# Griffin trunk layer on one core: three tiles for the gate chain, earlier steps for h, and m5 ahead of m4 in the last stage

## The chip, the cores and the metric

The kernel runs on one core of one Trainium2 chip. The metric is device time in microseconds (us), the median of several executions. The page of the profile is of one execution.

## The reference

DEPTH is 1, so only the first kind of layer runs, a Griffin recurrent block, on 1024 tokens of width 2048. Cut to what is computed:

```python
u = rmsnorm(x, norm_pre)
proj = u @ w_in                      # (1024, 2048) @ (2048, 4096)
xb, gate = proj[..., :2048], proj[..., 2048:]
xc = causal_depthwise_conv4(xb) + conv_b
r = sigmoid(blockdiag(xc, w_r) + b_r)   # 8 blocks of 256 x 256
i = sigmoid(blockdiag(xc, w_i) + b_i)
log_a = -8 * r * softplus(-lam);  a = exp(log_a)
b = sqrt(-expm1(2 * log_a)) * (i * xc)
h_t = a_t * h_{t-1} + b_t            # scan over the tokens
y = (h * silu(gate)) @ w_out
h = x + rmsnorm(y, norm_post)
out = h + sigmoid(h @ w_gate) * (p @ w_ple)
```

## The kernel before

All tensors lie with features on partitions and tokens along the row, in two halves of 512 tokens (h = 0 and 1 in the names). Every float32 product is made of three matmuls of 128x512 on split operands (`mm3`, lines 116 to 118: hi x hi, hi x lo, lo x hi). A split is one ScalarE (ACT) copy into `whi` or the hi half of an operand (line 106) and one VectorE (DVE) subtraction into `wlo` or the lo half (line 107).

The three large products (x with `w_in`, y with `w_out`, h with `w_gate`) go by Winograd's form of Strassen's scheme: seven products m1 to m7 for each block p of 128 output rows. One product of one block is a **unit**, 8 x 3 = 24 matmuls on TensorE (PE). `grouped` and `led` write out the order of the units: m1 and m2, then m7, m6, m3 in groups of four, then m4 and m5, where `led(a, b, 2, ...)` gives b a lag of two blocks behind a. In the last stage m4 yields one tile of the output (i = 1, h = 0) and m5 two (h = 1), in `emit_out`. m4 reads the operand t4, m5 reads t1; both are differences of spilled tiles that `h_one` loads, subtracts and splits.

The program is a list of steps. `now[0]` counts units. Each unit has stages that are issued some units ahead: LOAD (7 ahead for m5 and m7, 4 for m1, m2 and m4), ADD (a weight block added onto the loaded one by a DMA on the GpSimd (POOL) queue, 5 ahead) and PART (the split, 3 ahead). `hook` and `spread` put other steps behind a unit of a stage, `do` behind the unit that stands before it. `later(k, f)` and `put(key, d, src, k)` issue a store to DRAM k units later on the POOL queue. SP and POOL run in the order in which this is written; from the y stage's third quarter on ACT and DVE do too (`begin_by_hand`), before that a scheduler sets their order and PE's. Each engine and queue works strictly in its order, so an instruction that waits holds up all behind it.

Tiles come from pools: `pairs` (13 buffers: raw weights, sums, output operands), `vecs` (7 buffers of 128x512: `one`), `acts` (24 split operands), and 8 PSUM banks.

**The chain.** For each of 8 blocks n and each half h, `block_conv` makes xc and its split x2, four banks of `ri` matmuls follow (`mm_ri`, a unit of its own), and `chain` makes r, i, a, b and the scan from them. One tile `rq` of 128x3x1024 holds R, I and Q (Q ends as the scan's states). There is one buffer of it. For h = 0 the states are stored by `put(..., 6)` (names `sp<-rq`), for h = 1 they are multiplied with the gate tile g (line 348).

**From y to h.** After the last y products come eight units `ple` (p with `w_ple`, 24 matmuls each, evacuated by ACT into `vecs` tiles pp, line 722, and stored). `h_first(n)` loads two z tiles and x, its use scales and adds them (`make_h`, lines 654 and 656, tile zr), stores the result and splits it into the operands b11 and b21 (names h_b) one unit later. h's first unit, m1 of block 0, reads all eight. `norm_z(step, 1)` is the second half's norm: its step 2 puts eight small matmuls on PE (`rb_z`).

Of the kernel before, what the change touches and what calls it, by code (L numbers as in the profile page):

```python
# [34 lines left out]
def trunk_kernel(ctx, tc, xT, pT, par, w_in, w_ri, w_out, w_gate, w_ple, out):  # L35
# [160 lines left out]
    def later(k, f):  # L196
        late.setdefault(now[0] + k, []).append(f)
# [115 lines left out]
        chain(h, n, banks)  # L313

    def chain(h, n, banks):
        rq = chain_tile("rq", f"rq{h}_{n}", (P, 3, 2, T))
        R, I, Q = (rq[:, j] for j in range(3))
        A2 = st.pop(("xc", h, n))
        for s in range(2):
            ct = 2 * n + s  # L320
            nc.scalar.activation(R[:, s], banks[0][s], AF.Sigmoid, bias=col(C_BR, ct))  # L321
            nc.scalar.activation(I[:, s], banks[1][s], AF.Sigmoid, bias=col(C_BI, ct))
        nc.vector.tensor_tensor(I, I, A2, ALU.mult)
        for s in range(2):
            nc.scalar.activation(Q[:, s], R[:, s], AF.Tanh, scale=dk[:, 0, 2 * n + s : 2 * n + s + 1])

        for s in range(2):
            ct = 2 * n + s
            nc.scalar.activation(R[:, s], R[:, s], AF.Exp, scale=dk[:, 1, ct : ct + 1])
        nc.scalar.activation(R, R, AF.Square)  # L330
        nc.scalar.activation(R, R, AF.Square)
        nc.scalar.activation(A2, R, AF.Square)
        nc.vector.scalar_tensor_tensor(Q, A2, 1.0, Q, op0=ALU.add, op1=ALU.mult)
        root = nc.scalar.activation(Q, Q, AF.Sqrt)
        if h == 1:
            later(2, lambda: open_gates(root.ins))
        nc.vector.tensor_tensor(I, I, Q, ALU.mult)
        for s in range(2):
            ct = 2 * n + s
            init = 0.0 if h == 0 else hcar[:, ct : ct + 1]  # L340
            nc.vector.tensor_tensor_scan(Q[:, s], R[:, s], I[:, s], init, ALU.mult, ALU.add)
        if h == 0:
            nc.vector.tensor_copy(hcar[:, 2 * n : 2 * n + 2], Q[:, :, T - 1])
            for s in range(2):
                put(2 * n + s, hs, Q[:, s], 6)
        else:
            g = gs.pop(n)
            nc.vector.tensor_tensor(g, Q, g, ALU.mult)
            for s in range(2):
                put((("b12", "b22")[s], n), yd, g[:, s], 5)  # L350

# [138 lines left out]
    def strassen(key, w, orders, emit, hooks, early=None, park=False, inserts=()):  # L492
# [14 lines left out]
        def mm(u, p, name):  # L507
# [7 lines left out]
            if name == "m1":  # L515
                banks[p] = b
                if park:
                    m1 = one(f"m1{key}{p}")
                    nc.scalar.activation(m1, b, AF.Copy)
                    put(p, parked, m1, 2)  # L520
                else:
                    u_tile(p)
                    nc.scalar.activation(us[key, p][:, 0], b, AF.Copy)
# [59 lines left out]
    def x_mm(u, p, name):  # L583
# [23 lines left out]
        elif name == "m4":  # L607
# [3 lines left out]
            def gated():  # L611
                nc.scalar.activation(g, g, AF.Silu)
                nc.vector.tensor_tensor(g, g, h0.pop(p), ALU.mult)  # L613
                put((("b11", "b21")[s], n), yd, g)

            gate(gated, p >= NK - 4)
        elif name == "m5":
# [115 lines left out]
    def emit_out(p, i, h, b, part):  # L733
        dt = 2 * p + i
        o, sg = outs.pop((dt, h)), one(f"sg{dt}_{h}")
        if part is None:
            nc.scalar.activation(sg, b, AF.Sigmoid)
        else:
            nc.vector.tensor_tensor(sg, part, b, ALU.subtract if h == 0 else ALU.add)  # L739

        def rest():
            if part is not None:
                nc.scalar.activation(sg, sg, AF.Sigmoid, scale=-1.0 if (i, h) == (0, 1) else 1.0)
            nc.vector.tensor_tensor(sg, sg, o[:, 0], ALU.mult)
            nc.vector.tensor_tensor(sg, sg, o[:, 1], ALU.add)  # L745
            later(1, lambda: nc.gpsimd.dma_start(out[h, :, dt, :], sg))  # L746

        return rest

# [134 lines left out]
    for i in range(3):  # L884
        hook(i, lambda i=i: norm_z(i, 0))
    spread(1, 2, [lambda n=n: h_first(n) for n in range(3)], 2)
    hook(4, lambda: load_p(0))
    hook(5, lambda: load_p(1))
    strassen("y", w_out, [(p, "m5") for p in range(NB)], emit_z, hooks)
    uses = {}  # L890
    for i in range(KH):
        plain(w_ple[i], f"ple{i}", lambda u, i=i: mm_ple(u, i), 512)
        for f in uses.pop(i, ()):
            do(f)
        if i < 5:
            got = []
            do(lambda got=got, i=i: got.append(h_first(i + 3)))
            uses.setdefault(i + 2, []).append(lambda got=got: got.pop()())
        if i < 3:
            do(lambda i=i: norm_z(i, 1))  # L900


    orders, o2, o3 = grouped(range(NB), range(NB), led("m4", "m5", 2, range(NB)))
    hooks = {}
    spread(0, 1.5, [lambda n=n: h_second(n) for n in range(KH)], 2)
    spread(o2 - 1, 0.75, fetches("h", hold, "t2"), 2)
    spread(o2 + 2, 0.75, [lambda n=n: fetch("h", {("b22", k): hd[1, 2 * k + 1] for k in (n, n + 1)}, "b22", n) for n in range(0, KH, 2)], 2)
    spread(o3 - 8, 0.5, [lambda n=n: h_one("t4", n) for n in range(KH)], 2)
    spread(o3 - 4, 0.5, [lambda n=n: h_one("t1", n) for n in range(KH)], 2)
    strassen("h", w_gate, orders, emit_out, hooks, early_out, True)  # L910


# [97 lines left out]
```

## Time and profile before

| | us |
|---|---|
| median of 3 runs (1418.79 to 1422.9) | 1420.37 |
| the profiled execution, its own time | 1417.82 |
| its span, first to last instruction | 1416.0 |
| PE busy | 1380.6 |
| DVE busy | 947.1 |
| ACT busy | 729.5 |
| POOL busy | 271.8 |

Time is lost where PE, in its order, waits; so the table is read together with the list of PE's waits and the stretches around them. The profiled execution is 2.55 us below the median.

### The profile page before, as it was taken

To read this page: it belongs to the slowest core of one execution; us is meant where nothing else is said; L and a number is where in the kernel's file an instruction comes from. 1 tells how busy PE (TensorE), PEld (TensorE's weight loads), DVE (VectorE), ACT (ScalarE), POOL (GpSimd) and SP (SyncE) were. 2 spreads that over 40 slices of the span, in tenths; PEclk is the share of its full clock that TensorE was granted. 3 is DMA by queue.
4 is the path that set the end of the run, shared out by engine and by line. 5 is a ranking of instruction groups with operands and counts; after the bars stand their busy time and mean duration, and the time that the engine had idled before them with its cause. 6 is when DMAs were issued, how large, how long until landed. Compare 5 with 4: busy or idle time off the path is not lost. (4 is left out here: it accounts for less than half of the span.)

```text
span 1416.0 us, 17194 instructions
## 1 busy us (share of the span) xinstructions
PE 1380.6 (97%) x6025; PEld 1128.1 (80%) x6025; DVE 947.1 (67%) x1255; ACT 729.5 (52%) x960; POOL 271.8 (19%) x422
## 2 busy tenths in 40 slices
PE   9999999999999999999999999999999899999997
PEld 6888778778887878888787788888887788888786
DVE  8588678557575656588789855355676586626867
ACT  8332256666666643789898652224345333423423
POOL 0003331112121111011102331102114233110122
PEclk9999999999999999999999999999999999999999
DMA  9778898768777798468776999757589999986995
GB/s 353 241 241 305 297 308 241 217 157 225 186 173 207 189 327 253 159 189 269 242 249 257 336 311 301 186 150 212 131 298 349 325 356 330 301 225 170 317 351 201
DMA packets 126391, 358.81 MB, mean 253 GB/s; under 512 B 15968, under 2 KB 16352, under 8 KB 126304
## 3 DMA queue, kind: packets, MB, share of 16 engines
q1 hardware_dynamic: 83808, 210.88, 42.1%
q0 software_dynamic: 42496, 146.83, 40.0%
q8 instruction: 47, 0.77, 0.2%
q14 instruction: 40, 0.33, 0.1%
HBM read 277.95 MB, written 79.69 MB: 253 GB/s over the span
## 5 line engine op out<-in xcount | busy, mean ns | idle before, releaser
L436 POOL DMA_DIRECT2D x_m<-in_w_in x64 | 57.8, 964 | 190.5 <-DVE wlo_x10m L107 21.1
L294 DVE SCALAR_TENSOR_TENSOR xc<-xbp,cst,xc 128x512 f32<-128x512 f32 x96 | 66.8, 743 | 1.0 <-ACT xc L291 0.9
L436 POOL DMA_DIRECT2D h_m<-in_w_gate x32 | 28.6, 894 | 139.4 <-DVE h_t L107 22.9
L117 PE MATMUL ri<-x,whi_ri 128*128 128x512 f32 x128 | 51.8, 405 | 1.8 <-DVE x L107 1.6
L116 PE MATMUL ri<-x,whi_ri 128*128 128x512 f32 x128 | 49.7, 408 | 3.7 <-ACT x L106 3.7
L118 PE MATMUL ri<-x,wlo_ri 128*128 128x512 f32 x128 | 51.3, 401 | 0.0
L206 POOL DMA_DIRECT2D sp<-g x32 | 17.9, 574 | 164.4 <-DVE g L613 137.0
L321 ACT ACT_TABLE_LOAD x16 | 20.5, 1283 | 51.2 <-DMA sp<-rq 35.0
L436 POOL DMA_DIRECT2D y_m<-in_w_out x32 | 28.3, 895 | 79.5 <-DVE wlo_y4m L107 16.5
L106 ACT ACTIVATE x<-xc 128x1024 fp32r<-128x1024 f32 x16 | 16.8, 1053 | 32.6 <-DVE xc L294 32.6
L116 PEld LDWEIGHTS ri<-x,whi_ri 128*128 128x128 f32 x128 | 24.5, 194 | 10.7 <-ACT x L106 5.0
L291 ACT ACTIVATE xc<-xbp,cst 128x512 f32<-128x512 f32 x32 | 24.4, 806 | 15.5 <-DMA xbp<-sp 12.0
L117 PEld LDWEIGHTS ri<-x,whi_ri 128*128 128x128 f32 x128 | 24.7, 193 | 9.4 <-DVE x L107 3.5
L746 POOL DMA_DIRECT2D out_t<-sg x32 | 18.0, 562 | 69.2 <-DVE sg L745 68.3
L118 PEld LDWEIGHTS ri<-x,wlo_ri 128*128 128x128 f32 x128 | 24.5, 192 | 5.9
L722 ACT ACTIVATE pp<-pp 128x512 f32<-128x512 f32 x32 | 18.1, 596 | 20.7 <-DMA sp<-pp 13.1
L106 ACT ACTIVATE x_t<-xu 128x512 fp32r<-128x512 f32 x8 | 5.0, 630 | 43.1 <-DVE xu L362 43.1
L206 POOL DMA_DIRECT2D sp<-ux x16 | 9.7, 605 | 89.8 <-DVE ux L605 89.6
L107 DVE TENSOR_TENSOR x_t<-fxt,x_t 128x512 fp32r<-128x512 f32 x24 | 15.9, 687 | 16.3 <-ACT x_t L106 16.3
L106 ACT ACTIVATE x_t<-fxt 128x512 fp32r<-128x512 f32 x24 | 14.2, 622 | 23.2 <-DMA fxt<-sp 23.2
L116 PE MATMUL pp<-p,whi_ple 128*128 128x512 f32 x64 | 25.1, 392 | 0.0
L117 PE MATMUL pp<-p,whi_ple 128*128 128x512 f32 x64 | 24.9, 389 | 0.0
(719 smaller groups left out, 4907.3 us busy)
## 6 DMA issues: line engine op xcount, KB each, us to landing
x_m<-in_w_in SPq DMA_DIRECT2D x72, 512.0 KB, 5.8
x_m<-in_w_in POOLq DMA_DIRECT2D x64, 512.0 KB, 7.6
y_m<-in_w_out SPq DMA_DIRECT2D x40, 512.0 KB, 6.7
h_m<-in_w_gate SPq DMA_DIRECT2D x40, 512.0 KB, 8.3
y_m<-in_w_out POOLq DMA_DIRECT2D x32, 512.0 KB, 8.3
o<-sp SPq DMA_DIRECT2D x64, 256.0 KB, 7.7
h_m<-in_w_gate POOLq DMA_DIRECT2D x32, 512.0 KB, 8.6
raw_ri<-in_w_ri SPq DMA_DIRECT2D x16, 512.0 KB, 6.1
```

The costliest lines, as they stand in the source:

```text
L106: nc.scalar.activation(hi, src, AF.Copy)
L107: nc.vector.tensor_tensor(lo, src, hi.bitcast(F32), ALU.subtract)
L116: nc.tensor.matmul(ps, whi, ahi, start=start, stop=False, skip_group_check=more)
L117: nc.tensor.matmul(ps, whi, alo, start=False, stop=False, skip_group_check=more)
L118: nc.tensor.matmul(ps, wlo, ahi, start=False, stop=stop, skip_group_check=more)
L206: nc.gpsimd.dma_start(t, src)
L291: nc.scalar.activation(xc[:, s], xbp[:, s, 3 : T + 3], AF.Identity, bias=col(C_CB, ct), scale=col(C_CW + 48, ct))
L294: nc.vector.scalar_tensor_tensor(xc[:, s], xbp[:, s, j : j + T], col(C_CW + 16 * j, ct), xc[:, s], op0=ALU.mult, op1=ALU.add)
L321: nc.scalar.activation(R[:, s], banks[0][s], AF.Sigmoid, bias=col(C_BR, ct))
L436: nc.gpsimd.dma_start(u["raw"], w[(p, *ADDED[name])], accum_op=ALU.add)
L722: nc.scalar.activation(t, b, AF.Copy)
L746: later(1, lambda: nc.gpsimd.dma_start(out[h, :, dt, :], sg))
```

## The change

1. `chain` takes three tiles (`rr`, `ri`, `rq`) for R, I and Q in place of one. They have the same total size, one buffer each.
2. Stores move to later units: of g of the chain from 5 to 6 for blocks 0 to 5, of m1 of the y and h stages (`parked`) from 2 to 3, of the gated g of m4 in the x stage from 1 to 3 for p below 12.
3. `h_first` for n = 3 and 4 is issued within the y stage (hooks 6 and 7) and used behind ple units 0 and 1. Each use issues the load of n + 2. So all of n = 3 to 7 stand two units earlier. `norm_z(1, 1)` stays behind ple unit 1, its last step (`rb_z`) moves from behind unit 2 to behind unit 3.
4. In the last stage `led("m5", "m4", ...)`: m5 of block p now leads m4 by two blocks. `h_one("t1")` is spread from o3 - 10, `h_one("t4")` from o3 - 6 (o3 is the number of the stage's first m4 or m5 unit); before, t4 from o3 - 8 and t1 from o3 - 4.
5. The last stores of the output (blocks 6 and 7, of m4 and m5) are issued on SP in place of POOL.

```diff
     def chain(h, n, banks):
-        rq = chain_tile("rq", f"rq{h}_{n}", (P, 3, 2, T))
-        R, I, Q = (rq[:, j] for j in range(3))
+        R, I, Q = (chain_tile(t, f"{t}{h}_{n}") for t in ("rr", "ri", "rq"))
         A2 = st.pop(("xc", h, n))
...
-                put((("b12", "b22")[s], n), yd, g[:, s], 5)
+                put((("b12", "b22")[s], n), yd, g[:, s], 6 if n < NB - 2 else 5)
...
-                    put(p, parked, m1, 2)
+                    put(p, parked, m1, 3)
...
-                put((("b11", "b21")[s], n), yd, g)
+                put((("b11", "b21")[s], n), yd, g, 3 if p < NK - 4 else 1)
...
-            later(1, lambda: nc.gpsimd.dma_start(out[h, :, dt, :], sg))
+            later(1, lambda: (nc.sync if p >= NB - 2 and i + h else nc.gpsimd).dma_start(out[h, :, dt, :], sg))
...
     spread(1, 2, [lambda n=n: h_first(n) for n in range(3)], 2)
+
+    uses, got_h = {}, {}
+    for n in range(3, KH):
+        uses[n - 3] = lambda n=n: (got_h.pop(n)(), got_h.__setitem__(n + 2, h_first(n + 2)) if n + 2 < KH else None)
+    for n in (3, 4):
+        hook(n + 3, lambda n=n: got_h.__setitem__(n, h_first(n)))
     hook(4, lambda: load_p(0))
     hook(5, lambda: load_p(1))
     strassen("y", w_out, [(p, "m5") for p in range(NB)], emit_z, hooks)
-    uses = {}
     for i in range(KH):
         plain(w_ple[i], f"ple{i}", lambda u, i=i: mm_ple(u, i), 512)
-        for f in uses.pop(i, ()):
-            do(f)
-        if i < 5:
-            got = []
-            do(lambda got=got, i=i: got.append(h_first(i + 3)))
-            uses.setdefault(i + 2, []).append(lambda got=got: got.pop()())
-        if i < 3:
-            do(lambda i=i: norm_z(i, 1))
-
-
-    orders, o2, o3 = grouped(range(NB), range(NB), led("m4", "m5", 2, range(NB)))
+        if i in (0, 1, 3):
+            do(lambda i=i: norm_z(min(i, 2), 1))
+        if i in uses:
+            do(uses[i])
+
+
+    orders, o2, o3 = grouped(range(NB), range(NB), led("m5", "m4", 2, range(NB)))
...
-    spread(o3 - 8, 0.5, [lambda n=n: h_one("t4", n) for n in range(KH)], 2)
-    spread(o3 - 4, 0.5, [lambda n=n: h_one("t1", n) for n in range(KH)], 2)
+    spread(o3 - 10, 0.5, [lambda n=n: h_one("t1", n) for n in range(KH)], 2)
+    spread(o3 - 6, 0.5, [lambda n=n: h_one("t4", n) for n in range(KH)], 2)
```

ACT's order at the start of the chain of block 3, second half, before the change; rq holds R, I and Q, ri are the banks, g the gates.

```order
L106 ACTIVATE whi_x11m_5213<-x_m_5020 128x1024
L321 ACT_TABLE_LOAD
L321 ACTIVATE rq_3_5301<-ri_3_00_5273,cst 128x512
L321 ACTIVATE rq_3_5301<-ri_3_01_5274,cst 128x512
L612 ACT_TABLE_LOAD
L612 ACTIVATE g_12_5198<-g_12_5198 128x512
L106 ACTIVATE whi_x14m_5269<-x_m_5208 128x1024
L322 ACT_TABLE_LOAD
L322 ACTIVATE rq_3_5301<-ri_3_10_5275,cst 128x512
L322 ACTIVATE rq_3_5301<-ri_3_11_5276,cst 128x512
L325 ACTIVATE rq_3_5301<-rq_3_5301,dk 128x512 x2
L329 ACT_TABLE_LOAD
```

The same place in the changed kernel, where rr is R, ri_3_5320 is I, ri_3_00 to ri_3_11 are still the banks and rq is Q:

```order
L106 ACTIVATE whi_x11m_5231<-x_m_5036 128x1024
L320 ACT_TABLE_LOAD
L320 ACTIVATE rr_3_5319<-ri_3_00_5291,cst 128x512
L611 ACT_TABLE_LOAD
L611 ACTIVATE g_12_5216<-g_12_5216 128x512
L106 ACTIVATE whi_x14m_5287<-x_m_5226 128x1024
L321 ACT_TABLE_LOAD
L321 ACTIVATE ri_3_5320<-ri_3_10_5293,cst 128x512
L320 ACTIVATE rr_3_5319<-ri_3_01_5292,cst 128x512
L321 ACTIVATE ri_3_5320<-ri_3_11_5294,cst 128x512
L324 ACTIVATE rq_3_5321<-rr_3_5319,dk 128x512 x2
L328 ACT_TABLE_LOAD
```

The work is the same; the first instruction that writes Q's tile now is the tanh, behind all four sigmoids.

DVE's order around the first ple units before the change; zr is the tile of `make_h`, h_b its split operand, n_z the norm's small tiles.

```order
L107 TENSOR_TENSOR h_b_8358<-zr_8210,h_b_8358 128x512
L107 TENSOR_TENSOR h_b_8361<-zr_8210,h_b_8361 128x512
L126 TENSOR_SCALAR n_z_8374<-ss_z_8369 128x4
L107 TENSOR_TENSOR wlo_ple_8431<-raw_ple_8316,whi_ple_8430 128x512
L131 RECIPROCAL n_z_8376<-n_z_8375 128x4
L132 TENSOR_TENSOR n_z_8377<-n_z_8376 128x4
L133 TENSOR_TENSOR n_z_8377<-n_z_8377,n_z_8374 128x4
L134 TENSOR_SCALAR n_z_8377<-n_z_8377 128x4
L135 TENSOR_TENSOR n_z_8376<-n_z_8376,n_z_8377 128x4
L107 TENSOR_TENSOR wlo_ple_8491<-raw_ple_8380,whi_ple_8490 128x512
L654 SCALAR_TENSOR_TENSOR zr_8364<-zr_8364,cst,rstd_z_8062 128x512 x2
L656 TENSOR_TENSOR zr_8364<-zr_8364,xr_3_8365 128x1024
```

The same place in the changed kernel:

```order
L107 TENSOR_TENSOR h_b_8403<-zr_8242,h_b_8403 128x512
L126 TENSOR_SCALAR n_z_8411<-ss_z_8406 128x4
L653 SCALAR_TENSOR_TENSOR zr_8302<-zr_8302,cst,rstd_z_8094 128x512 x2
L655 TENSOR_TENSOR zr_8302<-zr_8302,xr_3_8303 128x1024
L107 TENSOR_TENSOR wlo_ple_8476<-raw_ple_8358,whi_ple_8475 128x512
L107 TENSOR_TENSOR h_b_8479<-zr_8302,h_b_8479 128x512
L107 TENSOR_TENSOR h_b_8482<-zr_8302,h_b_8482 128x512
L131 RECIPROCAL n_z_8413<-n_z_8412 128x4
L132 TENSOR_TENSOR n_z_8414<-n_z_8413 128x4
L133 TENSOR_TENSOR n_z_8414<-n_z_8414,n_z_8411 128x4
L134 TENSOR_SCALAR n_z_8414<-n_z_8414 128x4
L135 TENSOR_TENSOR n_z_8413<-n_z_8413,n_z_8414 128x4
```

Block 3's zr steps and splits moved ahead of the norm's chain from line 131 on; the norm's chain keeps its unit.

ACT's order at the start of the last stage before the change; h_t1k is the split of t1 of block k, whi_h0m5 the weights of m5 of block 0, sg the outputs.

```order
L106 ACTIVATE whi_h0m5_10563<-h0_m5_10331 128x1024
L743 ACTIVATE sg1_0_10561<-sg1_0_10561 128x512
L106 ACTIVATE h_t12_10570<-ht1_2_10420 128x512
L106 ACTIVATE h_t13_10573<-ht1_3_10423 128x512
L106 ACTIVATE whi_h3m4_10609<-h3_m4_10531 128x1024
L743 ACTIVATE sg3_0_10607<-sg3_0_10607 128x512
L106 ACTIVATE h_t14_10616<-ht1_4_10472 128x512
L106 ACTIVATE h_t15_10619<-ht1_5_10475 128x512
L106 ACTIVATE whi_h1m5_10663<-h1_m5_10431 128x1024
L743 ACTIVATE sg5_0_10661<-sg5_0_10661 128x512
L106 ACTIVATE h_t16_10670<-ht1_6_10519 128x512
L106 ACTIVATE h_t17_10673<-ht1_7_10522 128x512
```

The splits of t1 in the changed kernel:

```order
L106 ACTIVATE h_t12_10334<-ht1_2_10204 128x512
L106 ACTIVATE h_t13_10337<-ht1_3_10207 128x512
L106 ACTIVATE whi_h6m3_10378<-h6_m7_9908 128x1024
L106 ACTIVATE h_t14_10382<-ht1_4_10245 128x512
L106 ACTIVATE h_t15_10385<-ht1_5_10248 128x512
L106 ACTIVATE whi_h7m3_10423<-h7_m7_9942 128x1024
L106 ACTIVATE h_t16_10427<-ht1_6_10294 128x512
L106 ACTIVATE h_t17_10430<-ht1_7_10297 128x512
L106 ACTIVATE whi_h0m5_10476<-h0_m5_10252 128x1024
```

All of t1 now stands ahead of the split of m5's first weights; before, six of its eight splits stood behind it.

## Rows read from the trace of the kernel before

**Rows 1.** The page, part 1: busy us, share of the span, instructions.
```profile
PE 1380.6 (97%) x6025; PEld 1128.1 (80%) x6025; DVE 947.1 (67%) x1255; ACT 729.5 (52%) x960; POOL 271.8 (19%) x422
```

**Rows 2.** Waits of PE: who waited for whom, us in total, times, longest.
```profile
PE ri L116 <- ACT x L106: 3.7, 3, 2.9
PE hm L116 <- ACT h_b L106: 3.2, 1, 3.2
...
PE rb_z L141 <- ACT pp L722: 2.2, 1, 2.2
...
PE ri L117 <- DVE x L107: 1.6, 2, 1.2
PE hm L117 <- DVE h_t L107: 1.4, 1, 1.4
...
PE hm L117 <- DVE h_b L107: 0.8, 1, 0.8
...
PE hm L116 <- ACT h_t L106: 0.5, 1, 0.5
```

**Rows 3.** Windows: PE, PEld, DVE, ACT, POOL busy (count), PEclk, DMA share, GB/s.
```profile
686.30:692.10 5.80, 5.80 (x14) 4.54 (x15) 5.80 (x7) 2.86 (x4) 0.00 (x0) 0.50 0.45 95
1102.70:1108.90 6.20, 6.20 (x15) 4.85 (x16) 1.74 (x2) 1.54 (x2) 0.90 (x2) 0.51 0.95 328
1110.00:1116.20 6.20, 6.20 (x29) 5.15 (x28) 1.23 (x1) 1.55 (x2) 0.54 (x1) 1.00 0.93 282
```

**Rows 4.** Groups of ACT: busy, mean ns, idle before, what ended it.
```profile
L321 ACT ACTIVATE rq<-ri,cst 128x512 f32<-128x512 f32 x32 | 20.9, 686 | 0.2
L321 ACT ACT_TABLE_LOAD x16 | 20.5, 1283 | 51.2 <-DMA sp<-rq 35.0 <-DVE g L348 16.2
```

**Rows 5.** Timeline of PE, first half's chains: start us, duration [idle before, releaser].
```profile
270.50 0.50 PE L118 MATMUL xm<-x_t,wlo_x4m 128*128 128x512 f32 x1 [2.25 <-DVE wlo_x4m L107]
293.54 0.50 PE L118 MATMUL xm<-x_t,wlo_x7m 128*128 128x512 f32 x1 [0.52 <-DVE wlo_x7m L107]
312.71 0.50 PE L118 MATMUL xm<-x_t,wlo_x6m 128*128 128x512 f32 x1 [1.63 <-DVE wlo_x6m L107]
450.87 0.50 PE L118 MATMUL xm<-x_t,wlo_x15m 128*128 128x512 f32 x1 [1.14 <-DVE wlo_x15m L107]
```

**Rows 6.** Timeline of DVE and ACT, second half, start of block 3's chain.
```profile
655.09 2.46 DVE L341 TENSOR_TENSOR_SCAN rq<-rq,hcar 128x512 f32<-128x512 f32 x2
658.04 1.22 DVE L348 TENSOR_TENSOR g<-rq,g 128x1024 f32<-128x1024 f32 x1
659.36 1.28 ACT L321 ACT_TABLE_LOAD   x1 [1.43 <-DVE g L348]
```

**Rows 7.** Timeline of DVE, PE and ACT around the ple units.
```profile
1064.68 0.16 DVE L135 TENSOR_TENSOR n_z<-n_z,n_z 128x4 f32<-128x4 f32 x1
1064.99 1.13 PE L141 MATMUL rb_z<-ident,n_z 128*128 128x128 f32 x8 [2.23 <-ACT pp L722]
1098.18 1.23 DVE L656 TENSOR_TENSOR zr<-zr,xr 128x1024 f32<-128x1024 f32 x1
1100.63 1.16 ACT L106 ACTIVATE h_b<-zr 128x512 fp32r<-128x512 f32 x2
```

**Rows 8.** Timeline of ACT, last stage.
```profile
1331.42 1.06 ACT L106 ACTIVATE whi_h3m<-h_m 128x1024 fp32r<-128x1024 f32 x1 [5.07 <-DMA h_m<-in_w_gate]
```

**Rows 9.** Timeline of POOL: the last two stores.
```profile
1411.02 0.54 POOL L746 DMA_DIRECT2D out_t<-sg  x1 [3.44 <-DVE sg L745]
1412.35 0.54 POOL L746 DMA_DIRECT2D out_t<-sg  x1 [0.79 <-DVE sg L745]
```

**Rows 10.** Waits of POOL, a DMA issue, and ACT's timeline: what bounds the new waits.
```profile
POOL sp L206 <- ACT m1y L519: 26.9, 4, 11.5
...
sp<-pp POOLq DMA_DIRECT2D x32, 256.0 KB, 6.5
...
1084.81 1.31 ACT L722 ACTIVATE pp<-pp 128x512 f32<-128x512 f32 x2 [3.44 <-DMA sp<-pp]
```

## Prediction

> **What bounds the kernel now.** Read the page's first part: PE is busy for 97% of the span [rows 1], so only time in which PE waits, or runs slowly, can be won. The list of PE's waits [rows 2] shows few of them, and the change touches the places of nearly all that stand in it. The windows [rows 3] add what that list leaves out: behind the two longest waits, PE issued 14 matmuls in 5.80 us and 15 in 6.20 us at a granted clock of 0.50 and 0.51, against 29 in 6.20 us at 1.00 a little later. So a long wait costs twice: its length, and then 5.80 - 14 x 6.20/29 = 2.8 us, or 6.20 - 15 x 6.20/29 = 3.0 us, at the lower of the clock's two levels. Whoever counts waits alone misses nearly half.
>
> **Three tiles, first half.** ACT's sigmoid group [rows 4] shows where chains start late: the table load at line 321 waits 51.2 us in all, 35.0 of them for `sp<-rq`, the store of the last chain's states out of the one tile. With a tile of its own for R and I, the table load (1.28 us) and the sigmoids need no store; only the tanh on Q does, behind four sigmoids (4 x 0.69). Some of these may lie elsewhere in ACT's order, so I count the table load and two sigmoids that go ahead of the wait: 1.28 + 2 x 0.69 = 2.7 us earlier for all that is queued on ACT behind the chain, and for DVE behind that. PE feels it through the weight splits. Its waits on DVE in these chains are 2.25, 0.52, 1.63 and 1.14 us [rows 5]. The last three are shorter than 2.7, so they should go: 3.3 us. The first hangs, in DVE's queue, on the landing of another tile as well; I count nothing for it (bounds 0 and 2.25). Term: -3.0, between 0 (below, first rival) and -5.5.
>
> **Three tiles, second half.** Here no store reads the tile; the product with g (line 348) does, and the chain's table load waits 16.2 us for it [rows 4]. R and I need only that the last scan be done. At block 3's chain, the scan ends at 655.09 + 2.46 = 657.55 and the product at 659.26, and ACT waited 1.43 us [rows 6]: all of that goes, up to 1.7 us a chain, and it adds up, since each chain starts behind the last. PE waited in this half for x from ACT, 3.7 us in three waits, and for x from DVE, 1.6 us in two [rows 2]: 5.3 us. The order shown of this chain leaves the work the same, so I count 3.8 of the 5.3; if the 2.95 us wait shrinks so far that the clock stays up, 2.8 us more. Term: -6.6, between 0 and -8.1.
>
> **Steps for h.** PE's first m1 unit waited 3.2 us for the last h_b from ACT and 0.8 us from DVE [rows 2]. Its source: zr of block 7 was done only at 1098.18 + 1.23 = 1099.41, and its hi split began at 1100.63 [rows 7]. In the changed kernel these steps stand two units earlier, which is some 2 x 24 x 6.20/29 = 10.3 us [rows 3] of order. Not all of it arrives, since the steps wait in turn (next term), but 3.2 + 0.8 us is less than half. So both waits go, and the stretch at the lower clock that follows them: 4.0 + 3.0 = 7.0.
>
> The wait of `rb_z`, 2.2 us, is put down to ACT's pp. But what these matmuls need last is n_z, and DVE wrote that from 1064.68, right ahead of rb_z at 1064.99 [rows 7]. The norm's chain keeps its unit on DVE, and PE has one more unit of 5.1 us ahead of rb_z: a slack of 5.1 - 2.2 = 2.9 us in place of the wait. Ahead of the norm's chain stand now two zr steps and two h_b splits (the order shown); zr's last step took 1.23 us [rows 7], so I estimate 4 us for all. What of that falls into time in which DVE waited for the ple split that stands among them is free. I take the 2.2 as gone; 1.1 of it (4 - 2.9) could stay.
>
> What is late next: the store of zr and the pp stores share POOL's queue and `vecs`. A pp store takes 6.5 us from issue to landing, and ACT already waited 3.44 us for one at 1084.81 [rows 10]. With the z, x and zr tiles of blocks 3 to 7 taken earlier, the last ple units can find no vecs buffer, so that their banks are evacuated late. I price this as a new wait of PE of 2.2 us, between 0 and 5. Sum of this part: -7.0 - 2.2 + 2.2 = -7.0, between -9.2 and -3.1.
>
> **Last stage.** ACT waited 5.07 us for a load of weights at 1331.42 [rows 8] with the splits of t1 queued behind it (the order shown: six of eight stood behind m5's first weights). PE waited for h_t twice, 0.5 and 1.4 us [rows 2]. Now all t1 splits stand ahead of those weights, and t4 has its two blocks of lag. Term: -1.9, between 0 and -1.9. What becomes tighter is SP: m5's units come first and take their loads early, and t1's and t4's tiles with them (rival below).
>
> **End.** Before, the last unit is an m5, which yields two outputs; POOL stored them at 1411.02 and 1412.35 [rows 9]. After, the last unit is m4 with one output. So the last store is issued 1412.35 - 1411.02 = 1.3 us earlier, and that is the end of the span. The stores of the last blocks move to SP, whose queue is empty of loads by then. A POOL issue is shown as 0.54 us [rows 9]; what SP's takes here no row shows. I take 0.2 less, between 0 and 0.54 (a store that SP issues later than POOL would have to stand behind a load, and none is left). Term: -1.5, between -1.3 and -1.9.
>
> The Trainium skill, "Trainium Kernel Development and Optimization", section "Key Constraints", speaks against this last edit: queues issued from SP, ACT and POOL run on the same sixteen DMA engines, and using several saves only issue time. By it the edit is worth no more than the issue. The sum keeps 0.2 either way, and no run of before has a last store on SP to show it.
>
> **Later stores.** Each holds its `vecs` tile one unit longer (g of the chain, m1) or two (g of m4), 5.1 us a unit. In return POOL, whose order holds all adds and stores, no longer stands at a store whose data isn't there: it waited 26.9 us in four waits for m1y alone, 11.5 in one [rows 10]. PE shows no wait on an add in [rows 2], so this gain hides behind the adds' lead. Against it stands a pool of seven: a tile held longer blocks ACT's next evacuation or SP's next load. I take +3, between 0 and +8 (about half a unit for one or two places).
>
> **The sum.** -3.0 - 6.6 - 7.0 - 1.9 - 1.5 + 3 = -17.0, against the profiled execution's 1417.8: 1400.8. That execution lies 2.55 us below the median of the runs, so on the scale of the median about 1403. Within 0.3%, or 4.3 us, is what a measurement of this kernel hardly tells from no change.
>
> **Rivals.**
>
> *Three tiles give nothing (0.17).* The tanh on Q waits for the same store or product; if ACT stands there as long less the sigmoids, and what PE waits for is queued behind the tanh, each chain ends when it ended before. For it: the waiting instruction is still in the chain, and ACT's order is fixed, so all behind it waits as before. Against it: the sigmoids and a table load no longer lie behind the wait, and in the second half the scan ended 1.7 us ahead of the product [rows 6]. It takes 9.6 from the sum: 7.4 us gained, 1413.
>
> *The last stage collides (0.08).* With m5 first, its raw weights, the tiles for t1 and the loads for t4 meet in SP's queue and the 13 buffers of `pairs`. ACT's wait of 5.07 us for a load [rows 8] shows that SP is late there already. If that wait comes back ahead of the splits of t1 for m5's first unit, PE waits about as long, 5 us, and then runs at the lower clock for 3 more [rows 3]; one or two such: 8 to 14 us of the gain go, 1409 to 1415 or so.
>
> *Tiles held too long: slower (0.06).* m1's evacuation on ACT frees the bank that PE writes next, and takes a tile of `vecs`. If at each m1 y unit the pool is empty until the store, now a unit later, has landed (6.5 us for a store like it [rows 10]), ACT stands up to 5.1 us there, and PE with it once its banks are full. At five of the eight blocks' m1 that is 26 us against the 20.0 that the other terms gain: 1420 + 6 = 1426. It decides from four such waits on. Against it: ACT's own idle time and PE's free banks take up a wait of a few us, and POOL stood waiting for m1y, so a store so far came before its data, not behind it.
>
> *A gain larger than forecast (0.10).* The 2.25 us of [rows 5], all of the second half's waits, and later stores that cost nothing: 1395 to 1398.
>
> *The waits only shift (0.05).* Each wait that goes is taken by the next instruction in order, so that the sum comes out within 4.3 us of before.
>
> The forecast itself has 0.54: 1398 to 1408, which takes in the bounds of +3 and of the new ple wait. The range of 8 in 10 goes from 1395 to 1416, which reaches over the first rival and the collision. Faster by over 0.3% is below 1416.1: the forecast, the larger gain, nearly all of the first rival and the collision, less what their own spread puts above: 0.83. Within 0.3%: 0.10. Slower: 0.07.
>
> **What would show it.** Three tiles: the table load of the chain no longer waits for `sp<-rq` or for g; that wait is on line 324 instead and shorter by the sigmoids' time; PE's waits of 0.52, 1.63 and 1.14 us on those weight splits are gone, and the stretch that answers to the one at 686 has a clock of 1.00. Steps for h: no wait on h_b in the first h unit, no clock of 0.51 behind it, rb_z without a wait; a wait on pp's banks in the last ple units of at most some 2 us. Last stage: no wait on h_t. End: the last store on SP, about 1.5 us earlier from PE's last matmul. Later stores: POOL's wait for m1y shorter, and new waits for `sp<-` stores on ACT or SP. It is wrong if PE's waits reappear at the same units for another releaser, or if ACT's waits on stores grow by more than the sigmoids gave back.

## The result and the profile after

| | before | changed |
|---|---|---|
| median of 3 runs, us | 1420.37 | 1398.05 (1395.33 to 1401.1) |
| ratio of the two, 95% interval | | 0.9839 (0.9817 to 0.9861) |
| the profiled execution, its own time, us | 1417.82 | 1401.1 |
| its span, us | 1416.0 | 1399.3 |
| PE busy, us | 1380.6 | 1374.3 |

The change gains 1.6%: by the ratio 1420.37 x 0.0161 = 22.9 us, interval 19.7 to 26.0. The forecast was a gain of 17.0, 1403 us in a range of 1395 to 1416. The profiled execution of before is 2.55 us below its median, that of after 3.05 above its own, so the two spans lie only 16.7 us apart; where the other 6 us are is said at the end. Five more runs of the changed kernel (e9 below) gave a ratio of 0.9858 (0.9836 to 0.9879), 20.2 us.

PE's waits in the changed kernel (who waited for whom, total us, times, longest), which answer to [rows 2]:

```profile
PE xm L118 <- DVE wlo_x15m L107: 4.0, 1, 4.0
PE pp L116 <- ACT pp L721: 3.8, 4, 2.0
PE ri L116 <- ACT x L106: 2.9, 1, 2.9
PE xm L118 <- DVE wlo_x4m L107: 1.6, 1, 1.6
...
PE xm L118 <- DVE wlo_x6m L107: 1.2, 1, 1.2
PE ri L117 <- DVE x L107: 1.1, 3, 0.4
...
PE hm L117 <- DVE h_t L107: 0.5, 1, 0.5
```

The waits on h_b and rb_z are gone. In their place stand 3.8 us on the banks of pp. The wait on h_t that is left lies at 1201 us, far from the last stage; those of the last stage are gone. Of the waits on weight splits in [rows 5], those of 0.52 and 1.14 us are gone and 2.25 and 1.63 have become 1.56 and 1.16. The wait for x in the second half, 2.9 us, is as long as before. The longest of all, 4.0 us for `wlo_x15m`, is at 164 us, where the change moves nothing. DVE's timeline there (start, duration, [idle before, releaser]) shows what it hangs on:

```profile
165.69 0.75 DVE L381 SCALAR_TENSOR_TENSOR xt<-xt,cst,rstd_x 128x512 f32<-128x512 f32 x1 [9.66 <-DMA xt<-in_xT]
166.36 0.68 DVE L579 TENSOR_TENSOR xb<-xm,rstd_x 128x512 f32<-128x512 f32 x1
166.96 1.22 DVE L107 TENSOR_TENSOR wlo_x15m<-x_m,whi_x15m 128x1024 fp32r<-128x1024 f32 x1
```

A load of x landed late, and in DVE's order the weight split stands two places behind the step that waits for it. This is a part of the spread between executions, not of the change (more at the end).

ACT's groups in the chain (busy, mean ns, idle before them, what ended it), the answer to [rows 4]:

```profile
L324 ACT ACTIVATE rq<-rr,dk 128x512 f32<-128x512 f32 x32 | 22.7, 719 | 18.2 <-DMA sp<-rq 18.2
L320 ACT ACTIVATE rr<-ri,cst 128x512 f32<-128x512 f32 x32 | 21.1, 687 | 2.0 <-PE ri L118 1.8
L320 ACT ACT_TABLE_LOAD x16 | 20.5, 1283 | 4.9 <-DVE rq L340 4.7
```

The table load's 51.2 us of waiting have become 4.9, now for the scan of the last block. The wait for the states' store went to the tanh (line 324), as forecast, and is half as long: 18.2 for 35.0. In single chains, two of the seven waits are gone and five are shorter by 2.5 to 3.7 us.

Three windows (us, busy PE, PEld, DVE, ACT, POOL with counts, PEclk, DMA share, GB/s) answer to [rows 3]: behind the wait for x, the first units of h, and the second half's chains.

```profile
680.90:686.70 5.80, 5.80 (x18) 4.62 (x19) 5.80 (x6) 3.39 (x4) 0.78 (x2) 0.71 0.30 78
1102.00:1108.00 6.00, 6.00 (x28) 4.96 (x27) 3.66 (x4) 2.83 (x3) 0.00 (x0) 1.00 1.03 412
600.00:800.00 200.00, 195.24 (x845) 159.00 (x844) 174.19 (x211) 179.59 (x223) 37.35 (x63) 0.99 0.78 260
```

In the first, PE still falls to the lower level for a part of the stretch: mean granted clock 0.71 in place of 0.50 (the lower of the two levels, 1.2 of 2.4 GHz), 18 matmuls in place of 14. In the second, the clock is 1.00 where it was 0.51. The third suggests why the wait for x stays: DVE is busy for 174 and ACT for 180 of 200 us there (tested in e11).

The end, on PE, DVE and SP's queue:

```profile
1392.93 0.39 PE L118 MATMUL hm<-h_t,wlo_h7m 128*128 128x512 f32 x1
...
1395.46 0.69 DVE L744 TENSOR_TENSOR sg<-sg,o 128x512 f32<-128x512 f32 x1
1396.18 0.33 SPq L745 DMA_DIRECT2D out_t<-sg  x1
```

From the end of the last matmul to the end of the span it is 1399.3 - 1393.32 = 6.0 us. Before, the last matmul ended at 1407.50 + 0.39, 8.1 us ahead of the end:

```profile
1407.50 0.39 PE L118 MATMUL hm<-h_t,wlo_h7m 128*128 128x512 f32 x1
```

### The profile page after: what moved, and what is told of

Its sections match the earlier page's. It is cut to its first block, busy times and chain, and to the rows that moved or that the text cites. A ratio compares the mean times of both kernels' runs of the same rounds, so it can differ in the third digit from the quotient of the medians.

```text
span 1399.3 us, 17187 instructions
## 1 busy us (share of the span) xinstructions
PE 1374.3 (98%) x6025; PEld 1126.3 (80%) x6025; DVE 946.8 (68%) x1255; ACT 732.0 (52%) x960; POOL 268.9 (19%) x416
## 4 chain that ended last, share of the span: by engine, by line
PE 65%; DMA 11%; DVE 10%; issue 8%; ACT 4%; POOL 2%; SPq 0%; DVEq 0%; POOLq 0%; ACTq 0%
PE xm L118 9%; PE xm L116 9%; PE xm L117 9%; PE ym L118 6%; PE ym L116 6%; PE ym L117 6%; PE hm L117 5%; PE hm L118 5%; PE hm L116 5%; DMA h_m<-in_w_gate 4%; POOL sp L206 2%; PE ri L118 2%; PE ri L117 2%; PE ri L116 1%; DMA sp<-pp 1%
## 5 line engine op out<-in xcount | busy, mean ns | idle before, releaser
L435 POOL DMA_DIRECT2D y_m<-in_w_out x32 | 28.9, 913 | 75.2 <-DVE wlo_y4m L107 16.7
L324 ACT ACTIVATE rq<-rr,dk 128x512 f32<-128x512 f32 x32 | 22.7, 719 | 18.2 <-DMA sp<-rq 18.2
L721 ACT ACTIVATE pp<-pp 128x512 f32<-128x512 f32 x32 | 18.1, 597 | 21.9 <-DMA sp<-pp 17.1
L116 PE MATMUL pp<-p,whi_ple 128*128 128x512 f32 x64 | 25.6, 400 | 3.8 <-ACT pp L721 3.8
L742 ACT ACTIVATE sg<-sg 128x512 f32<-128x512 f32 x24 | 14.3, 624 | 25.0 <-DVE sg L738 25.0
L107 DVE TENSOR_TENSOR x_t<-fxt,x_t 128x512 fp32r<-128x512 f32 x24 | 15.8, 688 | 16.0 <-ACT x_t L106 16.0
L745 POOL DMA_DIRECT2D out_t<-sg x26 | 15.1, 580 | 59.7 <-DVE sg L744 59.1
L106 ACT ACTIVATE whi_ri<-raw_ri 128x1024 fp32r<-128x1024 f32 x16 | 16.8, 1052 | 16.4 <-PE xm L117 12.5
```

What stands on the lines that cost most here:

```text
L106: nc.scalar.activation(hi, src, AF.Copy)
L107: nc.vector.tensor_tensor(lo, src, hi.bitcast(F32), ALU.subtract)
L116: nc.tensor.matmul(ps, whi, ahi, start=start, stop=False, skip_group_check=more)
L435: nc.gpsimd.dma_start(u["raw"], w[(p, *ADDED[name])], accum_op=ALU.add)
L721: nc.scalar.activation(t, b, AF.Copy)
L745: later(1, lambda: (nc.sync if p >= NB - 2 and i + h else nc.gpsimd).dma_start(out[h, :, dt, :], sg))
```

## Where the first half's gain comes from

The windows of both kernels over the chains, with the count of PE's matmuls, before first, then changed (its window from 600 us on stands above):

```profile
180.00:480.00 300.00, 293.82 (x1279) 238.76 (x1278) 191.43 (x238) 190.77 (x231) 59.64 (x81) 1.00 0.79 206
480.00:600.00 120.00, 118.03 (x519) 96.99 (x518) 73.11 (x95) 59.86 (x74) 14.38 (x21) 1.00 0.80 255
600.00:800.00 200.00, 193.76 (x830) 156.71 (x829) 171.79 (x206) 179.94 (x224) 34.62 (x58) 0.98 0.75 250
```

```profile
180.00:480.00 300.00, 297.27 (x1304) 244.21 (x1303) 199.15 (x248) 196.89 (x238) 61.90 (x84) 1.00 0.81 216
480.00:600.00 120.00, 119.58 (x527) 98.47 (x526) 72.12 (x92) 59.83 (x72) 14.24 (x22) 1.00 0.79 244
```

In the first half's stretch PE issued 25 matmuls more in the same time, in the next 8 more; at 6.20/29 us each [rows 3] that is 5.3 and 1.7 us. Between 600 and 800 it issued 845 for 830: 3.2 us. Each is a piece of the gain of one pair of executions. DVE's scans of blocks 0, 2, 4 and 7 show how the first of them arises, before and then changed:

```profile
228.71 2.33 DVE L341 TENSOR_TENSOR_SCAN rq<-rq 128x512 f32<-128x512 f32 x2
305.17 2.33 DVE L341 TENSOR_TENSOR_SCAN rq<-rq 128x512 f32<-128x512 f32 x2
375.12 2.33 DVE L341 TENSOR_TENSOR_SCAN rq<-rq 128x512 f32<-128x512 f32 x2
483.25 2.33 DVE L341 TENSOR_TENSOR_SCAN rq<-rq 128x512 f32<-128x512 f32 x2
```

```profile
229.16 2.33 DVE L340 TENSOR_TENSOR_SCAN rq<-rr,ri 128x512 f32<-128x512 f32 x2
302.84 2.34 DVE L340 TENSOR_TENSOR_SCAN rq<-rr,ri 128x512 f32<-128x512 f32 x2
370.45 2.33 DVE L340 TENSOR_TENSOR_SCAN rq<-rr,ri 128x512 f32<-128x512 f32 x2
476.02 2.33 DVE L340 TENSOR_TENSOR_SCAN rq<-rr,ri 128x512 f32<-128x512 f32 x2
```

The changed kernel is 0.45 us behind at the first scan and 2.3, 4.7 and 7.2 us ahead at the others. The delay of one chain was handed on to the next, and on to the fetches and splits that stand behind the last chain. ACT's order there shows the second: the fetch that the split of the weights `x2m` stands behind lands near 515 us before and near 508 us after (before first):

```profile
515.13 1.21 ACT L106 ACTIVATE x_t<-fxt 128x512 fp32r<-128x512 f32 x2 [7.75 <-DMA fxt<-sp]
```

```profile
507.90 1.15 ACT L106 ACTIVATE x_t<-fxt 128x512 fp32r<-128x512 f32 x2 [8.17 <-DMA fxt<-sp]
```

What that is worth, the trace of before understates. PE waits there for `x2m`'s two splits, 1.2 and 0.8 us in it. In the four later traces whose first half still waits as before (e2 to e5 below) the first of these waits is 2.3 to 3.4 us, and the clock falls behind it, to 0.94 to 0.97 in the mean of the stretch from 480 to 540 us. The windows of before, of e4, the longest, and of the changed kernel:

```profile
480.00:540.00 60.00, 58.02 (x255) 47.46 (x254) 38.77 (x52) 23.95 (x32) 10.06 (x15) 1.00 0.97 322
```

```profile
480.00:540.00 60.00, 56.36 (x236) 45.65 (x234) 38.52 (x51) 25.20 (x33) 8.56 (x13) 0.94 0.95 303
```

```profile
480.00:540.00 60.00, 60.00 (x267) 49.69 (x266) 36.40 (x50) 22.63 (x30) 9.20 (x14) 1.00 0.98 319
```

The five traces without the tiles' effect in the first half hold 255, 240, 243, 236 and 239 matmuls here, the nine with it 266 or 267. The difference of the means, 24 matmuls, is 5.1 us.

## The experiments

Each kernel ran five rounds against the kernel before on the same chip, 4 to 12 executions of it beside 8 to 29 of before, in three sets: e1 to e4, e5 to e8, e9 to e12. Gains are the ratio's distance from 1 times the median of before in that set, with the 95% interval.

| run | gain in us | interval |
|---|---|---|
| e1 three tiles alone | 13.8 | 10.5 to 17.1 |
| e2 later stores alone | -2.1 | -4.8 to 0.6 |
| e3 steps for h alone | 6.7 | 4.3 to 9.2 |
| e4 last stage and last stores alone | 3.8 | 1.4 to 6.1 |
| e5 three tiles, R's wait back in the first half | 3.4 | 1.4 to 5.4 |
| e6 three tiles, R's wait back in the second half | 11.1 | 8.8 to 13.4 |
| e7 changed, without the later stores | 21.2 | 18.3 to 24.2 |
| e8 changed, states stored a unit earlier | 21.9 | 18.5 to 25.3 |
| e9 changed, again | 20.2 | 17.2 to 23.3 |
| e10 changed, states earlier, no later stores | 22.6 | 19.3 to 25.8 |
| e11 changed, no root in the second half | 19.0 | 15.8 to 22.2 |
| e12 changed, last stores on POOL | 22.4 | 20.0 to 25.0 |

**The parts alone (e1 to e4).** Each is the kernel before with one part of the change's diff, which stands above. Theory A was that the parts add, and that the three tiles carry the gain in the chains; the rival gave it to the later stores.

e1, the first three lines of the diff:

> The kernel before with three tiles for R, I and Q and nothing else. Theory A, that the tiles carry the gain in the chains: the two traces put 8.7 us less lost time of PE between 165 and 520 us and 2.9 us less between 520 and 830, so 9 to 12 us faster, with no wait of the chain's table load on the states' store and the waits of PE on weight splits at 293 and 450 gone. Rival B, that the later stores on POOL carry it (POOL's wait for the gated g fell from 137.0 to 86.6 us): 0 to 3 us faster, and the waits of PE between 165 and 520 stay.

e2, item 2 of the change:

> The kernel before with the later stores of g of the chain, of m1 and of the gated g, and nothing else. Theory A (as on record, the term of the later stores): 3 us slower, between 0 and 8. Rival B: 6 to 9 us faster, because POOL no longer stands at stores whose data is not there and its adds and stores come sooner; then PE's waits at 270, 312 and 517 shrink without the tiles.

e3, item 3:

> The kernel before with the steps of h_first two units earlier and norm_z's last step one unit later, and nothing else. Theory A: the traces show 9.7 us of lost time of PE between 1050 and 1120 before and 4.1 after, the 4.1 being new waits for pp's banks in ple units 2 to 5; so 5 to 6 us faster, no wait on h_b, no clock of 0.51 behind it. Rival: without the later store of m1 the vecs buffers run out in another place, and the new waits are as long as the old: 0 to 2 us faster.

e4, items 4 and 5:

> The kernel before with m5 ahead of m4 in the last stage, the earlier steps for t1 and t4, and the last stores on SP, and nothing else. Theory A: the waits on h_t go (1.9 us and their overhead, 2.4 in the trace) and the end is 2.1 us shorter (8.1 to 6.0 us behind PE's last matmul): 4 to 4.5 us faster. Rival, the collision on SP: the changed trace has new waits of 0.5 us at 1169 and 1201 (1.9 us lost between 1120 and 1330), and if these come from the new order of the last stage, only 2 to 2.5 us faster.

They add: 13.8 - 2.1 + 6.7 + 3.8 = 22.2 us, beside 22.9 and 20.2 for all together. The rival of e1 and e2 fell: the later stores alone gain nothing, and in e1 the table load waits for no store and PE's waits at 293 and 450 us are gone. POOL's wait for the gated g fell from 137.0 us in the kernel before to 111.6 in e2, and the time did not. e1 gained more than theory A had read out of the traces (9 to 12), though its interval takes in a part of that. In e3, the waits on h_b are gone, the stretch behind them runs at a clock of 1.00, and 2.7 us of new waits stand on pp (changed kernel 3.8):

```profile
PE pp L116 <- ACT pp L722: 2.7, 3, 1.5
```

e4's trace ends 6.0 us behind the last matmul and has no wait on h_t, nor any other wait of over 0.2 us from 1110 us on, so the collision on SP, its rival, did not come. Its time alone doesn't decide: the interval of 1.4 to 6.1 takes in both forecasts.

**Which half (e5, e6).** The three tiles stay, but in one half R and Q change places from block to block, so that R again lands on the tile that holds the last states. For e5 (for e6, `h == 1`):

```diff
-        R, I, Q = (chain_tile(t, f"{t}{h}_{n}") for t in ("rr", "ri", "rq"))
+        names = ("rq", "ri", "rr") if h == 0 and n % 2 else ("rr", "ri", "rq")
+        R, I, Q = (chain_tile(t, f"{t}{h}_{n}") for t in names)
```

> Three tiles alone, but in the first half R and Q change tiles from block to block, so that R again lands on the tile whose states are being stored. Theory A (first half carries most of the 13.8 us of the three tiles, since each chain's delay is handed on to the next until the waits near 517 us): 2 to 4 us faster than the kernel before, with ACT's wait for the states' store back at line 321 and PE's wait at 517 back. Rival (the sum on record: first half 3.0, second half 6.6): 6 to 11 us faster than before.

> Three tiles alone, but in the second half R and Q change tiles from block to block, so that R again waits for the product of the states with g. Theory A: 10 to 11 us faster than the kernel before, 3 us less than with three tiles in both halves; PE's waits near 745 us are back. Rival (the sum on record): 3 to 5 us faster than before.

Theory A held in both: the first half alone gives 11.1 us, the second alone 3.4, together 14.5 for the 13.8 of both. In e5 ACT's chain waits again at line 321, 39.5 us, and PE's wait near 517 us is back (its list of waits):

```profile
L321 ACT ACT_TABLE_LOAD x16 | 20.5, 1283 | 39.5 <-DMA sp<-rr 20.4 <-DMA sp<-rq 14.4 <-DVE rq L341 4.6
```

```profile
PE xm L116 <- ACT whi_x2m L106: 2.7, 1, 2.7
```

One thing in e6 was not as expected. R waits 11.1 us for the product with g again, but PE's waits near 745 us did not come back. Its stretch from 600 to 800 us holds 844 matmuls, as many as the changed kernel's 845. In e5, where only the second half's wait is gone, the same stretch holds 842, against 830 before. So in the traces either edit alone brings nearly all of this stretch's gain, the first half's earlier chains as much as the second half's own wait, and what is credited to each half is not sharply parted; the times (11.1 and 13.8, intervals that overlap) don't part the two either.

**The later stores in the changed kernel, and the states' store (e7, e8, e10).** e7 is the changed kernel without item 2. e8 and e10 store the states earlier:

```diff
-                put(2 * n + s, hs, Q[:, s], 6)
+                put(2 * n + s, hs, Q[:, s], 5)
```

> The changed kernel without the later stores. Theory A (terms add; alone the later stores cost 2.1 us, interval -0.6 to 4.8): 0 to 4 us faster than the changed kernel, 1394 to 1398. Rival (the later stores pay only once the chains run earlier, since their data then stands ready and POOL's waits for the gated g fall): 2 to 5 us slower than the changed kernel, 1400 to 1403.

> The changed kernel with the states of the first half stored five units behind their chain in place of six. In the changed trace the scan ends 5 to 10 us before the store in all chains but the last, and the tanh still waits 18.2 us for that store in five chains, PE 1.6 and 1.2 us behind it. Theory A (the store's landing is what is left): the tanh waits at most 5 us in all, PE's waits at 270 and 310 go, 2 to 4 us faster than the changed kernel. Rival (POOL then stands at stores whose scan is not done and its adds come late; or other work than the tanh sets these waits): within 1 us of the changed kernel.

> The changed kernel with the states stored five units behind their chain and without the later stores. Theory A (the earlier store ends the tanh's waits, 3.5 us less lost between 165 and 480 in its trace, and the later stores gain nothing): 2 to 4 us faster than the changed kernel on this chip, tanh without waits for the states' store. Rival (with the old, earlier stores in POOL's queue the states' store is late again): within 1 us of the changed kernel.

e7 decides between neither: 21.2 us against the changed kernel's 22.9 and 20.2. POOL waits 137.6 us for the gated g again there, and the time is the same, so that this wait lies beside other work.

e8 did in the trace what theory A said. The tanh waits for no store (ACT's group):

```profile
L324 ACT ACTIVATE rq<-rr,dk 128x512 f32<-128x512 f32 x32 | 22.6, 718 | 0.0
```

PE's waits at 270 and 310 us are gone, and its window from 180 to 480 us holds 13 matmuls more than the changed kernel's 1304:

```profile
180.00:480.00 300.00, 299.74 (x1317) 246.52 (x1316) 204.93 (x256) 198.59 (x238) 63.00 (x85) 1.00 0.82 219
```

That is 2.8 us, and 4.5 against e9's 1296. But e10 speaks against the store as the only cause. There the tanh's wait is gone too (0.1 us), yet PE's wait near 268 us is 1.9, as in e7, and the window holds 1306 matmuls, 8 or 1.7 us more than in e7, which differs from e10 by the states' store alone:

```profile
180.00:480.00 300.00, 297.77 (x1306) 244.56 (x1305) 202.66 (x252) 198.81 (x239) 61.00 (x82) 1.00 0.82 217
```

What removed the wait near 270 us in e8 stays open. The times don't show a gain: the intervals of e8, e10, e9 and the changed kernel overlap. e8's median of 1395.88 lies below e7's 1398.06 and e10's 1397.54 below e9's 1400.16, but e12's 1397.40, without the earlier store, is as low as e10's. Both beat the kernel before; that either beats the changed kernel is not shown.

**The wait for x that stays (e11).** In the second half's chains the square root is left out for a square, so that ACT loads fewer tables:

```diff
-        root = nc.scalar.activation(Q, Q, AF.Sqrt)
+        root = nc.scalar.activation(Q, Q, AF.Sqrt if h == 0 else AF.Square)
```

> The changed kernel with a square in place of the square root in the second half's chains; the root is left out there. ACT then loads two tables fewer in each of the chains 0 to 5 or so (1.28 us each). Theory A (PE's wait of 2.9 us for x near 680 us, which three tiles left, is ACT's own load: ACT was busy without a gap there): that wait falls to 0 to 1 us, with the lower clock behind it gone, 3 to 5 us faster than the changed kernel. Rival (x is late because of DVE's six convolution steps, 4.06 us, or of a transfer): the wait stays at 2 us or more, within 1 us of the changed kernel.

PE's waits in it, and ACT's timeline ahead of the longer:

```profile
PE ri L116 <- ACT x L106: 5.5, 2, 5.0
```

```profile
706.33 1.13 ACT L624 ACTIVATE g<-g 128x512 f32<-128x512 f32 x2
707.37 2.17 ACT L106 ACTIVATE y_b<-fyb 128x512 fp32r<-128x512 f32 x4
709.45 1.04 ACT L106 ACTIVATE whi_y1m<-y_m 128x1024 fp32r<-128x1024 f32 x1
710.40 1.04 ACT L106 ACTIVATE x<-xc 128x1024 fp32r<-128x1024 f32 x1
```

Half of theory A held: two table loads of 1.28 us each stood ahead of x's split in the changed kernel (at 675.08 and 677.46 us), and without them the wait near 680 us fell from 2.9 to 0.4, so it was ACT's load. But the gain did not come. A chain later, ACT's order, which the scheduler made anew, put four splits of y's operand and one of weights ahead of x, and PE waited 5.0 us there. In this kernel, with ACT and DVE this full, the wait moved to the next chain.

**SP against POOL at the end (e9, e12).** e12 is the changed kernel with all last stores on POOL, e9 the changed kernel itself, on the same chip.

```diff
-            later(1, lambda: (nc.sync if p >= NB - 2 and i + h else nc.gpsimd).dma_start(out[h, :, dt, :], sg))
+            later(1, lambda: nc.gpsimd.dma_start(out[h, :, dt, :], sg))
```

> The changed kernel once more, to stand on one chip beside the next three. Theory A (the alone runs add: 13.8, 6.7 and 3.8 us gained, 2.1 lost, in all 22.2): 1397 to 1399, ratio near 0.984. Rival (the two profiled executions, 16.7 us apart, tell the true gain): 1402 to 1404, ratio near 0.988.

> The changed kernel with all last stores on POOL, as before. Both theories give under a us in the median; the profile tells: from the end of PE's last matmul to the end of the span it was 8.1 us before and 6.0 in the changed kernel. Theory A (as on record, 0.2 us for SP against POOL): 6.2 us. Rival 1 (POOL's issue of 0.54 us counts in full, and its wake-up on the wait adds to it): 6.5 to 7. Rival 2 (the Trainium skill's rule that the issuing queue saves issue time alone): at most 0.54 us more, 6.0 to 6.5.

e9's 1400.16 us and 0.9858 lie between theory A and its rival. The interval, 0.9836 to 0.9879, holds A's 0.984 and reaches to a hair from the rival's 0.988, so it settles little between them. The end of e12, from its timelines:

```profile
1388.18 0.39 PE L118 MATMUL hm<-h_t,wlo_h7m 128*128 128x512 f32 x1
...
1390.72 0.69 DVE L744 TENSOR_TENSOR sg<-sg,o 128x512 f32<-128x512 f32 x1
```

```profile
1391.71 0.54 POOL L745 DMA_DIRECT2D out_t<-sg  x1 [4.89 <-DVE sg L744]
```

Its span is 1395.4, so 1395.4 - 1388.57 = 6.8 us from the last matmul to the end, against 6.0 with SP: 5.97 to 6.04 in the seven traces that end so (changed, e4, e7 to e11). That is in the range of rival 1. The 0.85 us (6.83 - 5.98) come in three pieces: POOL issues 0.30 us behind DVE's last step (1391.71 - 1391.41), SP 0.03 (1396.18 - 1396.15), a difference of 0.27; the issue takes 0.54 for 0.33 us, 0.21; the rest, 0.36, lies between the end of the issue and the end of the span. The medians can't show 0.85 us (e12 gained 22.4, e9 20.2).

The Trainium skill, "Trainium Kernel Development and Optimization", section "Key Constraints", says that issuing from several engines at once saves only issue time; by these rows the issue is a quarter of the difference, and the measurement decides. The Trainium skill, "DMA: Bandwidth & Descriptors", section "Specifications", gives about 1 us to the first byte from POOL's path and 0.6 from SP's; the estimate from that, 0.4 us, agrees with the 0.36 here.

## Why the prediction was right, and what was mis-sized

The direction, the places and the range held. The sum held in part by luck: the first half gave 8.1 us more than its term and the second half 3.2 less. The median of 1398.05 stands at the low end of the forecast's 1398 to 1408, at the border of the rival "A gain larger than forecast", but not by the waits that this rival named: 0.7 of the 2.25 us went, and not all of the second half's. By the prediction's own terms:

| term | forecast, us | measured, us | from |
|---|---|---|---|
| three tiles, first half | -3.0 (0 to -5.5) | -11.1 | e6 |
| three tiles, second half | -6.6 (0 to -8.1) | -3.4 | e5 |
| steps for h | -7.0 (-3.1 to -9.2) | -6.7 | e3 |
| last stage and end | -3.4 | -3.8 | e4 |
| later stores | +3 (0 to +8) | +2.1, interval takes in 0 | e2 |

**Three tiles, first half,** is the term that was mis-sized, and by more than its bounds. The 2.7 us that it took from ACT's order came: five of the seven waits are shorter by 2.5 to 3.7 us, and the two short ones are gone. The step that failed is the price of that for PE: "The last three are shorter than 2.7, so they should go: 3.3 us." It took each chain by itself, and only the waits that one trace showed in [rows 5]. The sentence that "it adds up, since each chain starts behind the last" was written only for the second half, but holds in the first: the scans come up to 7.2 us ahead. And the waits behind the last chain, on the weights of `x2m` near 517 us, have no term in the sum. They are gone in e1 and e6 and back in e5, 2.7 us, and that stretch alone is worth some 5.1 us; the trace of before, from which the sum was worked out, had the shortest of these waits. Of the three waits counted, 0.52 and 1.14 went and 1.63 became 1.16. e6's 11.1 holds a part from beyond the first half, 14 matmuls or 3.0 us between 600 and 800 us.

**Three tiles, second half.** The mechanism was right (the table load's wait for g is gone), the size was not. The wait of 2.95 us for x did not shrink: 2.9 after, and 1.95 (5.80 - 18 x 6.20/29) of the 2.8 us at the lower clock stayed. e11 shows that wait to be ACT's own load, which the tiles don't lessen. The waits of 0.54 and 1.19 us of x near 745 are gone.

**Steps for h.** The waits on h_b and rb_z and the clock of 0.51 went as forecast. That rb_z had waited for n_z and not for pp, as the prediction read it, is what the lists of e1, e2, e5 and e6 say (1.5 to 1.7 us behind DVE's line 135). The new wait for pp's banks came where it was said: 3.8 us in the changed kernel's first trace, 1.5 in e9's, 2.7 in e3, for 2.2 forecast.

**Last stage and end.** The waits on h_t went, 1.9. The end is 2.1 us shorter for 1.5: the second output of the last unit gave its 1.3, and SP gave 0.85 in place of 0.2. The upper bound of 0.54 was too low, since it held the issue alone.

**Later stores.** Alone 2.1 us slower, with an interval that takes in 0; in the changed kernel (e7) no cost can be seen. Whether they cost at all stays open.

**The rivals.** "Three tiles give nothing" fell with e1. Its mechanism is in the trace, the tanh waits for the same store, but half as long. Where the rest of that wait is gone, the traces show 1.7 us (e10 against e7) to 4.5 us (e8 against e9) of PE's time for it. The collision of the last stage did not come (e4). Nor did tiles held so long that it would be slower: the change is faster, and its later stores alone cost 2.1 us (e2).

## What to carry to other kernels

A wait at the head of a repeated chain is not priced by the waits of the busy engine in that chain: here the delay was handed on from chain to chain, so compare where the last one ends and look at what stands behind it, in more than one trace. What a wait cost is given back only where the engines behind it have room; in e11, with ACT and DVE busy for 169 and 174 of 200 us (600 to 800), a later instruction in order took its place. A buffer that holds several values of a chain waits for its longest-lived one; give the value that is stored away a tile of its own, and then look at what still waits for that tile.

## What was not expected of the hardware

The queue of the last store made 0.85 us at the end of the span, of which the issue itself is 0.21; POOL also began 0.27 us later behind the same DVE step, and the span ended 0.36 later behind the issue. POOL's 0.30 us behind the DVE step stands alike in all seven traces that end on POOL.

What a long wait costs at the lower clock is not fixed by its length. Behind the wait for x near 680 us, 2.7 and 2.9 us in the two traces, PE issued 14 matmuls in 5.80 us at a clock of 0.50 in e7 and 25 at 1.00 in e9:

```profile
678.92:684.72 5.80, 5.80 (x14) 4.54 (x15) 5.80 (x6) 2.97 (x4) 0.79 (x2) 0.50 0.16 58
```

```profile
682.22:688.02 5.80, 5.80 (x25) 4.71 (x26) 5.80 (x6) 3.55 (x5) 0.78 (x2) 1.00 0.33 89
```

So "a long wait costs twice" was so in the trace that the prediction read and in most others, not in e9 and e12. Why stays open.

A load of x near 160 us, which no version touched, lands so differently from execution to execution that DVE waits for it 5.2 us in e12 and 9.66 in the changed kernel's profile, and PE behind it 0.6 and 4.0 us. That is as much as single edits here are worth. Between 160 and 180 us PE issued 74 matmuls in the trace of before and 61 in the changed kernel's, 2.8 us of difference that no edit made. Between 480 and 540 us, around the wait near 517, it issued 12 to 19 fewer in e2 to e5 than in the trace of before, 3.3 us in the mean, so that this trace of before was short of what the wait mostly costs. By this estimate the two places make up about 6 us, which is what one profile of each kernel, 16.7 us apart, lacks of the 22.9 that the runs told.
